# Sums of squares on all four column groups, and a shared copy out of PSUM, in a two-layer trunk with latent attention

## The chip, the cores and the metric

The kernel runs on one core of a Trainium2 chip. The metric is the device time of one execution in microseconds (us). TensorE is written PE below, VectorE DVE, ScalarE ACT, GpSimd POOL and the queue that issues most transfers SP.

## The reference

The kernel computes two layers of a residual trunk over 528 tokens (16 meta tokens, then 512), with 1024 channels. What matters here are the three root-mean-square norms at the head of each layer:

```python
h = rmsnorm(h_res, norm_gain[l])          # over 1024 channels
proj = h @ w_in[l]
u_pool, z_pool, c_q, c_kv, k_rope, z_mla, g_pool, g_mla = split(proj)
# c_kv: 256 channels
c_kv = rmsnorm(c_kv_raw, g_kva)
...
kv = (c_kv @ w_kv_b)
merged = sigmoid(g_pool) * y_pool + sigmoid(g_mla) * y_mla
h_res = h_res + merged @ w_out[l]
```

`rmsnorm(x)` is `x * rsqrt(mean(x * x) + 1e-6) * gain`.

## The kernel before

Channels lie on the 128 partitions and tokens along the free dimension, so that a sum over channels is a matmul with ones. The token axis of 528 is handled as two halves of 264 (`FULL`); in the second layer most products run only over the last 512 (`XTOK`).

**The stream of GEMM tiles.** All large products are split into three matmuls (high x high, high x low, low x high: lines 190 to 192) in float32r, with weights that ACT rounds (line 185, `whi`) and DVE subtracts (line 186, `wlo`). Weights come in chunks of 256 KB through three buffers each. `stream()` is a generator over the planned products; every `yield` returns the estimated time of the matmuls just emitted. Side work is put between them by hand: `fill_now(ns)` emits about `ns` nanoseconds of GEMM matmuls before the next side step is emitted. Lines 190 to 192 are therefore the ordinary matmuls of the text. A scheduler then orders each engine's instructions with a timing model of its own, so that the built order of an engine can differ a little from the order of emission.

**The norms.** The norm of x is not applied before the projection. The products run on the raw x (times gain), and `norm_sums` works out the reciprocal roots while the products go on. It is called once in each layer, after the two tiles of the kv latent (`ckv0`, `ckv1`):

- The squares of x lie in eight tiles `xsq[0..7]`, those of the latent in `csq[0..1]`, each 128x528. Line 363 sums them with f32 matmuls against 32 columns of ones. `tile_position` chooses one of four column groups of 32 (0, 32, 64, 96) of PE. Sums of x go to groups 0 (first half of the tokens) and 64 (second half), those of the latent to 32 and 96. There is one PSUM tile for each half.
- ACT copies the two sums out of PSUM (line 370, 64x264 each). DVE replicates the meta tokens' part (line 371).
- Five transposes (lines 375 and 376) turn the sums so that tokens lie on partitions; each moves 33 columns, of which the first and the last are used.
- DVE adds the epsilons (lines 381 to 383) and takes three Newton steps to the reciprocal root (lines 294 to 300), then splits it (lines 391 to 393).
- `rows` transposes it back (lines 404 to 407, the row transposes of the text), and ACT copies it into `kinv` (lines 409, 410).
- `spread` (line 286) replicates each root over 128 partitions with a matmul, and ACT copies it out (line 287): two halves of `rinv`, for x, and two halves of `cinv`, for the latent. The eviction of the first product that needs `rinv` is that of `u0` (line 491), the first that needs `cinv` is that of `k0` (line 574).

The matmul tiles in PSUM, these spreads among them, come from one pool of four banks (`mmt`), so that a spread may have to wait until ACT has copied an earlier one.

The rotary key's product (`kr_body`, line 430) is elsewhere in the layer; it uses all four column groups with 16 f32 matmuls of 264 columns, and one PSUM tile for each half.

The order of products after the sums is `cq1`, `cq2` (three `cq` tiles start a layer's queue, the first before the sums), `u0`, `k0`, `u1`, the rotary key, `k1`, and so on.

Of the kernel before, what the change touches and what calls it, by code (L numbers as in the profile page):

```python
# [9 lines left out]
F32 = mybir.dt.float32  # L10
# [3 lines left out]
AF = mybir.ActivationFunctionType  # L14
ALU = mybir.AluOpType
# [3 lines left out]
P = 128  # L19
DEPTH = 2  # L20
D = 1024
SEQ = 512
NM = 16
T = SEQ + NM
HALF = T // 2
# [46 lines left out]
def trunk(ctx, tc, xT, pos, win, wkr, wqb, wkb, wvb, wgr, wpu, wmu, wout, gains, const, yT):  # L72
    nc = tc.nc
    pe, act, dve, gp, sp = nc.tensor, nc.scalar, nc.vector, nc.gpsimd, nc.sync
# [5 lines left out]
    sm = ctx.enter_context(tc.tile_pool(name="sm", bufs=1))  # L80
# [5 lines left out]
    def nm(s):  # L86
        uid[0] += 1
        return f"{s}_{uid[0]}"

    def slot(tag, dt=F32, bufs=1, w=W):  # L90
        return sl.tile([P, w], dt, tag=tag, name=nm(tag), bufs=bufs)

    def tmp(w=W):
        return tp.tile([P, w], F32, tag="tmp", name=nm("tmp"), bufs=3)
# [4 lines left out]
    def mmt():  # L99
        return pp.tile([P, 512], F32, tag="mm", name=nm("mm"), bufs=4)  # L100

    def sct():
        return pp.tile([P, 512], F32, tag="S", name=nm("S"), bufs=3)
# [27 lines left out]
    ident = cst[:, C_ID:C_ID + P]  # L131
    ones = cp.tile([P, P], F32, name="ones")
# [109 lines left out]
    def step():  # L242
        c = next(main, None)
        if c is None:
            flush()
            return False
        clk[0] += c
        while pend and pend[0][0] <= clk[0]:
            pend.pop(0)[1]()
        return True  # L250
# [23 lines left out]
    def fill_now(ns):  # L274
        end = clk[0] + ns
        while clk[0] < end and step():
            pass
# [5 lines left out]
    def spread(dst, i):  # L283
        for a, b in FULL:
            ps = mmt()[:, :b - a]
            pe.matmul(ps, sel[0:34, i:i + 1].to_broadcast([34, P]), kinv[:, a:b], start=True, stop=True)
            act.activation(dst[:, a:b], ps, AF.Copy)

    def behind(ins, other):
        tc.add_manual_dep(ins.ins, other.ins.name,  # L290
                          mybir.DependencyInfo(mybir.DependencyClass.Sync, mybir.DependencyReason.DATA))

    def newton(y, a, t):
        dve.tensor_single_scalar(y.bitcast(I32), a.bitcast(I32), 1, op=ALU.logical_shift_right)
        dve.tensor_scalar(y.bitcast(I32), y.bitcast(I32), -1.0, float(0x5F3759DF), op0=ALU.mult, op1=ALU.add)
        dve.tensor_scalar(a, a, -0.5, None, op0=ALU.mult)
        for _ in range(3):
            dve.tensor_mul(t, y, y)
            dve.tensor_mul(t, t, a)
            dve.scalar_tensor_tensor(out=y, in0=t, scalar=1.5, in1=y, op0=ALU.add, op1=ALU.mult)  # L300
# [20 lines left out]
    class Layer:  # L321
# [32 lines left out]

        def norm_sums(self):
            fill_now(2600)
            ps = [mmt(), mmt()]
            for t, r, start, stop in [(self.xsq[k], 0, k == 0, k == 7) for k in range(6)] + [
                    (self.csq[0], 32, True, False), (self.xsq[6], 0, False, False),
                    (self.xsq[7], 0, False, True), (self.csq[1], 32, False, True)]:  # L360
                for s, (a, b) in enumerate(FULL):
                    r_ = r + 64 * s
                    mm = pe.matmul(ps[s][r_:r_ + 32, :HALF], ones[:, 0:32], t[:, a:b], start=start, stop=stop,  # L363
                                   tile_position=(0, r_))
                    if t is not self.csq[1]:
                        behind(mm, self.csq_last)
            sums = tmp()
            rep = sm.tile([64, 8, NM], F32, tag="rep", name=nm("rep"))
            for s, (a, b) in enumerate(FULL):
                act.activation(sums[0:64, a:b], ps[s][64 * s:64 * s + 64, :HALF], AF.Copy)  # L370
            dve.tensor_copy(rep, sums[0:64, 0:NM].unsqueeze(1).to_broadcast([64, 8, NM]))
            fill_now(2600)
            ps = mmt()[:, 0:165].rearrange("p (j c) -> p j c", c=33)
            for j in range(4):
                pe.transpose(ps[:, j, :], sums[0:33, NM + P * j:NM + P * (j + 1)], ident[0:33, 0:33])
            pe.transpose(ps[:, 4, :], rep[0:33].rearrange("p a b -> p (a b)"), ident[0:33, 0:33])
            na = sm.tile([P, 2, 5], F32, tag="na2", name=nm("na2"))
            nt = sm.tile([P, 2, 5], F32, tag="nt2", name=nm("nt2"))
            self.ninv = ny = sm.tile([P, 2, 5], F32, tag="ny2", name=nm("ny2"))
            self.eps = sm.tile([P, 5], F32, tag="eps", name=nm("eps"))  # L380
            dve.tensor_scalar(na[:, 0, :], ps[:, :, 0], 1.0 / D, EPS, op0=ALU.mult, op1=ALU.add)
            dve.tensor_scalar(self.eps, na[:, 0, :], EPS, None, op0=ALU.mult)
            dve.scalar_tensor_tensor(out=na[:, 1, :], in0=ps[:, :, 32], scalar=1.0 / 256, in1=self.eps,
                                     op0=ALU.mult, op1=ALU.add)
            newton(ny, na, nt)
            w = tmp()
            gp.memset(w[:, 0:170], 0.0)
            v = w[:, 0:170].rearrange("p (j c) -> p j c", c=34)
            nv = ny.rearrange("p a j -> p j a")
            nh = sm.tile([P, 5, 2], F32R, tag="nh", name=nm("nh"))  # L390
            dve.tensor_copy(nh, nv)
            dve.tensor_copy(v[:, :, 0:33:32], nh.bitcast(F32))
            dve.tensor_sub(v[:, :, 1:34:32], nv, nh.bitcast(F32))
            fill_now(8200)
            self.rows(v, 34, kinv)
            self.inv, self.cinv = slot("rinv"), slot("cq9")
            fill_now(1300)
            spread(self.inv, 0)
            spread(self.cinv, 1)
            self.st = [sct(), sct()]  # L400
# [719 lines left out]
```

## Time and profile before

| | |
|---|---|
| median of three runs | 800.36 us (799.65 to 800.38) |
| the profiled execution | 799.36 us |
| its span, first to last instruction | 797.6 us |
| PE busy | 790.3 us, 99% of the span |
| line 363, both layers | 80 records of 386 ns, 40 in each layer |
| granted PE clock | 1.00 |

How to read it: the span is what the engines' rows cover; the execution is 1.8 us longer. In the timeline a row gives the start, the time from the first start to the last end of the merged instructions, the engine, the line, the operation, output and inputs, sizes and count, and in brackets how long the engine stood idle before it and what released it. Matmuls overlap in the pipeline, so that the record of one (0.28 us for 264 columns) is longer than the step from one start to the next. Times are counted from the first instruction. DVE, ACT and POOL run beside PE; their time counts only where PE waits for it.

### The profile page before, as it was taken

How to read it: one execution, taken by the hardware profiler on the slowest of the kernel's cores; microseconds unless marked ns; L12 is line 12 of the kernel's file. 1: busy time of each engine (PE TensorE's matmuls, PEld its weight loads, DVE VectorE, ACT ScalarE, POOL GpSimd, SP SyncE). 2: the span in 40 equal slices, each digit the busy share in tenths (PEclk: the TensorE clock that was granted, in tenths of full speed). 3: DMA queues.
4: the chain of work that ended last, by engine and by line, in shares of the span. 5: the costliest groups of instructions: out<-in, count | busy, mean ns of one | idle time of the engine just before them, and what ended most of it. 6: DMA issues, size and time to landing. Idle time of an engine off the chain costs nothing.

```text
span 797.6 us, 14595 instructions
## 1 busy us (share of the span) xinstructions
PE 790.3 (99%) x5329; PEld 711.8 (89%) x5329; DVE 528.1 (66%) x1136; ACT 416.0 (52%) x943; POOL 194.4 (24%) x262
## 2 busy tenths in 40 slices
PE   9999999999999999999999999999999999999998
PEld 8889999999999999999997997877788888887887
DVE  5568767437689987685354686665467889665942
ACT  8455645644556665543354456446455666654421
POOL 1024404003333322142000163021024333410600
PEclk9999999999999999999999999999999999999999
DMA  6222233335233222324642222334252322222373
GB/s 241 74 70 91 72 100 90 110 86 146 79 88 89 79 67 67 89 87 145 179 142 73 73 88 87 94 84 119 81 165 89 101 83 78 71 70 77 93 225 105
DMA packets 48872, 80.71 MB, mean 101 GB/s; under 512 B 5904, under 2 KB 14480, under 8 KB 48800
## 3 DMA queue, kind: packets, MB, share of 16 engines
q1 hardware_dynamic: 48656, 79.52, 33.2%
q8 instruction: 42, 0.69, 0.4%
q10 hardware_dynamic: 144, 0.26, 0.1%
q14 instruction: 30, 0.25, 0.1%
HBM read 73.40 MB, written 4.23 MB: 97 GB/s over the span
## 4 chain that ended last, share of the span: by engine, by line
PE 96%; DMA 2%; ACT 1%; DVE 1%; issue 0%; POOL 0%; ACTq 0%; POOLq 0%
PE mm L190 28%; PE mm L192 27%; PE mm L191 27%; PE mm L805 2%; PE S L191 2%; PE S L192 2%; PE S L190 1%; PE o L811 1%; PE o L810 1%; PE mm L363 1%; PE S L472 1%; DMA xb<-xT 1%; DMA bc<-kdr 1%; PE mm L430 0%; DMA rinv<-win 0%; DMA raw<-wmu 0%
## 5 line engine op out<-in xcount | busy, mean ns | idle before, releaser
L190 PE MATMUL mm<-hh,whi 128*128 128x264 f32 (+2 forms) x1096 | 346.0, 318 | 0.5 <-ACT whi L185 0.3
L191 PE MATMUL mm<-hl,whi 128*128 128x264 f32 (+2 forms) x1096 | 343.4, 314 | 0.0
L192 PE MATMUL mm<-hh,wlo 128*128 128x264 f32 (+2 forms) x1096 | 342.1, 315 | 0.0
L186 DVE TENSOR_TENSOR wlo<-raw,whi 128x512 fp32r<-128x512 f32 (+2 forms) x251 | 186.5, 746 | 115.0 <-ACT whi L185 108.2
L185 ACT ACTIVATE whi<-raw 128x512 fp32r<-128x512 f32 (+2 forms) x251 | 150.2, 601 | 182.6 <-PE mm L191 136.9
L190 PEld LDWEIGHTS mm<-hh,whi 128*128 128x128 f32 x1096 | 205.6, 188 | 13.8 <-ACT racc L819 0.5
L191 PEld LDWEIGHTS mm<-hl,whi 128*128 128x128 f32 x1096 | 206.2, 188 | 12.2 <-issue 0.4
L192 PEld LDWEIGHTS mm<-hh,wlo 128*128 128x128 f32 x1096 | 205.0, 188 | 12.7 <-issue 0.4
L711 POOL TENSOR_TENSOR tmp<-kp,bc 64x528 f32<-64x528 f32 x16 | 24.5, 1530 | 115.0 <-DMA bc<-kdr 79.8
L550 POOL TENSOR_TENSOR racc<-racc,tmp 128x264 f32<-128x264 f32 (+1 forms) x15 | 14.1, 941 | 142.8 <-ACT tmp L549 142.7
L783 POOL TENSOR_TENSOR pm<-pa,rs 128x16 f32<-128x16 f32 x32 | 11.6, 363 | 143.9 <-DVE rs L778 143.9
L893 POOL TENSOR_TENSOR tmp<-tmp,xb 128x264 f32<-128x264 f32 (+1 forms) x24 | 27.1, 1152 | 58.1 <-DVE tmp L891 33.0
L739 DVE CUSTOM_DVE_ANT_0 S<-S,maskw,nqs 128x272 f32<-128x272 f32 (+4 forms) x80 | 38.4, 498 | 1.6 <-PE S L192 1.2
L746 ACT ACTIVATE cq<-S,bia 128x400 f32<-128x400 f32 (+2 forms) x48 | 24.6, 517 | 22.0 <-DVE bia L773 12.2
L190 PE MATMUL mm<-u,whi 128*128 128x264 f32 (+1 forms) x108 | 35.2, 326 | 0.0
L192 PE MATMUL mm<-cq,wlo 128*128 128x264 f32 (+1 forms) x108 | 34.8, 323 | 0.0
L192 PE MATMUL mm<-u,wlo 128*128 128x264 f32 (+1 forms) x108 | 34.8, 322 | 0.0
L191 PE MATMUL mm<-cq,whi 128*128 128x264 f32 (+1 forms) x108 | 34.7, 322 | 0.0
L190 PE MATMUL mm<-cq,whi 128*128 128x264 f32 (+1 forms) x108 | 34.7, 322 | 0.0
L281 DVE TENSOR_TENSOR tl<-mm,th 128x512 fp32r<-128x512 f32 (+1 forms) x64 | 29.3, 481 | 6.8 <-ACT th L280 5.8
L785 POOL TENSOR_TENSOR cq<-cq,rs 128x384 f32<-128x384 f32 (+1 forms) x32 | 32.4, 1012 | 0.0
L280 ACT ACTIVATE th<-mm 128x512 fp32r<-128x512 f32 (+1 forms) x64 | 25.5, 433 | 10.3 <-PE mm L805 10.0
(266 smaller groups left out, 1374.4 us busy)
## 6 DMA issues: line engine op xcount, KB each, us to landing
raw<-win SPq DMA_DIRECT2D x143, 256.0 KB, 2.6
raw<-wout SPq DMA_DIRECT2D x32, 256.0 KB, 3.1
bc<-kdr SPq DMA_DIRECT2D x16, 264.0 KB, 3.7
raw<-wpu SPq DMA_DIRECT2D x16, 256.0 KB, 2.7
raw<-wmu SPq DMA_DIRECT2D x16, 256.0 KB, 2.6
raw<-wqb SPq DMA_DIRECT2D x12, 256.0 KB, 2.7
tmp<-xT SPq DMA_DIRECT2D x16, 132.0 KB, 3.3
tmp<-scr SPq DMA_DIRECT2D x7, 256.0 KB, 3.5
```

What stands on the lines that cost most here:

```text
L185: act.activation(hi[:, :n], raw[:, :n], AF.Copy)
L186: dve.tensor_sub(lo[:, :n], raw[:, :n], hi[:, :n].bitcast(F32))
L190: pe.matmul(out, wh, xh, start=start, stop=False)
L191: pe.matmul(out, wh, xl, start=False, stop=False)
L192: pe.matmul(out, wl, xh, start=False, stop=stop)
L280: act.activation(hi[:, a:b], src, AF.Copy)
L281: dve.tensor_sub(lo[:, a:b], src, hi[:, a:b].bitcast(F32))
L711: gp.tensor_mul(kf[r0:r0 + 64, :], self.kp[r0:r0 + 64, :], bc[r0:r0 + 64, :])
L739: dve.tensor_tensor_reduce(out=sv, in0=sv, in1=mask, scale=nqs[:, i, h:h + 1], scalar=3e38, op0=ALU.add, op1=ALU.min, accum_out=bia[:, c:c ...
L746: act.activation(pv, sv, AF.Exp, scale=-1.0, bias=bia[:, i:i + 1], accum_out=rs[:, c:c + 1])
L785: gp.tensor_mul(pt[i][:, NM:], pt[i][:, NM:], rs[:, i:i + 1].to_broadcast([P, n - NM]))
L893: gp.tensor_add(t[:, :b - a], t[:, :b - a], self.am[m][:, a:b])
```

## The change

- The sums of x are dealt out over all four column groups by the number of the tile: even tiles to groups 0 (first half of the tokens) and 64 (second half), odd tiles to 32 and 96. The eight tiles share one PSUM tile `px`. The latent's two tiles are dealt out in the same way into a second PSUM tile `pc`, so that each sum now comes as two partial sums. The emission takes two tiles at a time and goes through the four groups in turn.
- ACT copies the sums of x to partitions 0 to 63 of `sums`, DVE those of the latent to partitions 64 to 127. The replication covers 128 partitions instead of 64.
- The five transposes move 97 columns instead of 33. The first four are made to wait for ACT's last copy.
- DVE adds the partial sums with two further small operations.
- In the first layer 3900 ns of GEMM matmuls instead of 2600 are emitted between the sums and the transposes (half of a 264-column GEMM tile more).

```diff
         def norm_sums(self):
             fill_now(2600)
-            ps = [mmt(), mmt()]
-            for t, r, start, stop in [(self.xsq[k], 0, k == 0, k == 7) for k in range(6)] + [
-                    (self.csq[0], 32, True, False), (self.xsq[6], 0, False, False),
-                    (self.xsq[7], 0, False, True), (self.csq[1], 32, False, True)]:
+            px, pc = mmt(), mmt()
+            runs = [(px, self.xsq[k], k, k < 2, k >= 6) for k in range(8)] + [(pc, self.csq[m], m, True, True) for m in range(2)]
+            for k in range(0, 10, 2):
                 for s, (a, b) in enumerate(FULL):
-                    r_ = r + 64 * s
-                    mm = pe.matmul(ps[s][r_:r_ + 32, :HALF], ones[:, 0:32], t[:, a:b], start=start, stop=stop,
-                                   tile_position=(0, r_))
-                    if t is not self.csq[1]:
-                        behind(mm, self.csq_last)
+                    for ps, t, m, start, stop in runs[k:k + 2]:
+                        g = 64 * s + 32 * (m % 2)
+                        mm = pe.matmul(ps[g:g + 32, :HALF], ones[:, 0:32], t[:, a:b], start=start, stop=stop,
+                                       tile_position=(0, g))
+                        if t is not self.csq[1]:
+                            behind(mm, self.csq_last)
             sums = tmp()
-            rep = sm.tile([64, 8, NM], F32, tag="rep", name=nm("rep"))
+            rep = sm.tile([P, 8, NM], F32, tag="rep", name=nm("rep"))
             for s, (a, b) in enumerate(FULL):
-                act.activation(sums[0:64, a:b], ps[s][64 * s:64 * s + 64, :HALF], AF.Copy)
-            dve.tensor_copy(rep, sums[0:64, 0:NM].unsqueeze(1).to_broadcast([64, 8, NM]))
-            fill_now(2600)
-            ps = mmt()[:, 0:165].rearrange("p (j c) -> p j c", c=33)
+                copied = act.activation(sums[0:64, a:b], px[64 * s:64 * s + 64, :HALF], AF.Copy)
+                dve.tensor_copy(sums[64:128, a:b], pc[64 * s:64 * s + 64, :HALF])
+            dve.tensor_copy(rep, sums[:, 0:NM].unsqueeze(1).to_broadcast([P, 8, NM]))
+            fill_now(2600 if self.l else 3900)
+            ps = mmt()[:, 0:485].rearrange("p (j c) -> p j c", c=97)
             for j in range(4):
-                pe.transpose(ps[:, j, :], sums[0:33, NM + P * j:NM + P * (j + 1)], ident[0:33, 0:33])
-            pe.transpose(ps[:, 4, :], rep[0:33].rearrange("p a b -> p (a b)"), ident[0:33, 0:33])
+                behind(pe.transpose(ps[:, j, :], sums[0:97, NM + P * j:NM + P * (j + 1)], ident[0:97, 0:97]), copied)
+            pe.transpose(ps[:, 4, :], rep[0:97].rearrange("p a b -> p (a b)"), ident[0:97, 0:97])
...
             dve.tensor_scalar(na[:, 0, :], ps[:, :, 0], 1.0 / D, EPS, op0=ALU.mult, op1=ALU.add)
+            dve.scalar_tensor_tensor(out=na[:, 0, :], in0=ps[:, :, 32], scalar=1.0 / D, in1=na[:, 0, :],
+                                     op0=ALU.mult, op1=ALU.add)
             dve.tensor_scalar(self.eps, na[:, 0, :], EPS, None, op0=ALU.mult)
-            dve.scalar_tensor_tensor(out=na[:, 1, :], in0=ps[:, :, 32], scalar=1.0 / 256, in1=self.eps,
-                                     op0=ALU.mult, op1=ALU.add)
+            for c in (64, 96):
+                dve.scalar_tensor_tensor(out=na[:, 1, :], in0=ps[:, :, c], scalar=1.0 / 256,
+                                         in1=self.eps if c == 64 else na[:, 1, :], op0=ALU.mult, op1=ALU.add)
```

In the changed file the lines after the diff stand four further down: the row transposes are lines 408 to 411, the copies into `kinv` lines 413 and 414, the spreads stay at 286 and 287, the transposes of the sums are lines 376 and 377, DVE's copies out of PSUM line 371, the replication line 372, and the additions of the epsilons and partial sums lines 382 to 387.

## The prediction

> **What bounds the kernel now.** I read the page first: busy shares and the chain that ended last.
>
> ```profile
> span 797.6 us, 14595 instructions
> ...
> PE 790.3 (99%) x5329; PEld 711.8 (89%) x5329; DVE 528.1 (66%) x1136; ACT 416.0 (52%) x943; POOL 194.4 (24%) x262
> ...
> PE 96%; DMA 2%; ACT 1%; DVE 1%; issue 0%; POOL 0%; ACTq 0%; POOLq 0%
> ```
>
> TensorE is busy nearly throughout and is 96% of the chain: time taken off its queue comes off the end, and work elsewhere costs only where TensorE waits for it. Next, the timeline of TensorE around the sums of squares of layer 0 (line 363), around the rotary key's matmuls (line 430), which already use four column groups, and around the spreads of the reciprocal roots (line 286) in both layers.
>
> ```profile
> 24.07 0.28 PE L192 MATMUL mm<-hh,wlo 128*128 128x264 f32 x1
> 24.28 1.97 PE L363 MATMUL mm<-cq,ones 128*32 128x264 f32 x16
> 26.09 1.95 PE L363 MATMUL mm<-q,ones 128*32 128x264 f32 x24
> 28.54 0.25 PE L375 MATMUL mm<-cst,tmp 33*128 33x33 f32 x1 [0.50 <-ACT tmp L370]
> 28.71 0.39 PE L190 MATMUL mm<-hh,whi 128*128 128x264 f32 x1
> 28.94 0.28 PE L191 MATMUL mm<-hl,whi 128*128 128x264 f32 x1
> ...
> 41.80 0.63 PE L286 MATMUL mm<-kinv,sel 34*128 34x264 f32 x3
> 42.91 0.39 PE L286 MATMUL mm<-kinv,sel 34*128 34x264 f32 x1 [0.48 <-ACT rinv L287]
> ...
> 56.37 0.28 PE L192 MATMUL mm<-hh,wlo 128*128 128x264 f32 x1
> 56.58 1.99 PE L430 MATMUL mm<-xb,raw 128*32 128x264 f32 x32
> 58.50 0.39 PE L190 MATMUL mm<-kh,whi 128*128 128x264 f32 x1
> 58.72 0.28 PE L191 MATMUL mm<-kl,whi 128*128 128x264 f32 x1
> ...
> 448.37 0.51 PE L286 MATMUL mm<-kinv,sel 34*128 34x264 f32 x2
> 448.81 0.39 PE L192 MATMUL mm<-hh,wlo 128*128 128x264 f32 x1
> 449.04 0.29 PE L190 MATMUL mm<-hh,whi 128*128 128x264 f32 x1
> ```
>
> Each f32 matmul is two records. To price an interruption I count from the last ordinary matmul before it to the second after it, less the ordinary cadence: 0.1215 us for 264 columns (66 steps from 31.80 to 39.84), 0.2315 us for 512. So line 430 takes 58.72 - 56.37 - 0.24 = 2.11 us for 16 matmuls. Line 363 in layer 1, where nothing is waited for, takes 3.89 us for 20 (426.77 to 431.12, less two steps of 0.23). Both fit one rule: 0.44 us for each matmul of the busiest column group plus 0.36 at the edges (4 x 0.44 and 8 x 0.44).
>
> **The change, part by part.**
>
> Column groups. Today groups 0 and 64 each take eight matmuls of x while 32 and 96 take two of the latent; afterwards each group takes five: 5 x 0.44 + 0.36 = 2.56 us, 1.33 less in each layer. Bounds: 16 to 20 in proportion to line 430 gives 2.64, so 2.4 to 2.9.
>
> The Trainium skill's page TensorEngine Tiling (Array Packing), section Overview (Theoretical Speedup), gives up to 2x for 64 and 4x for 32 columns. By that factor two groups becoming four would halve the 3.89 us, and the whole sum below would be 3.7 instead of 2.4 us. The rows speak for less: line 363 already puts its latent matmuls into the idle groups.
>
> The wait. In layer 0 the first transpose stands right behind the sums and waits 0.50 us for the ACT copy. In the changed kernel's built order it stands 24 ordinary matmuls later, the other four after two more. The sums end at 24.19 + 2.56 = 26.75 on the old clock; ACT's two copies (0.80 together) end near 27.5. DVE's two new copies of 64x264 I take at 0.43 each (a PSUM read of 128x264, line 491; bounds 0.22, the 64x128 copy of line 371, and 0.69), so they and the replication end by 28.0. The transposes come at 26.75 + 24 x 0.1215 = 29.67, so even copies of 0.69 stay hidden. The wait goes, 0.50. In layer 1 the copies end near 430.8 and the transposes come at 434.4; there was no wait.
>
> Transposes. Five of 33 columns in one group cost 0.63 (435.52 to 436.61, less two steps); the row transposes, four of 128 columns and one of 16, cost 0.66. The new width of 97 lies between. In layer 0 they were already split in two (0.25 and 0.56) and stay so: 0.30 and 0.60, +0.09. In layer 1 the built order puts one ordinary matmul between the first and the rest: 0.30 + 0.60 instead of 0.63, +0.27 (bounds +0.1 and +0.4).
>
> The Trainium skill's page TensorEngine Tiling, section Tiling Modes (Key Properties), says that a change of tiling mode drains the engine. It speaks against the new split and gives no time; the trace's price for entering and leaving is about 0.2 us.
>
> DVE's chain to the roots. It gains two small operations at 0.20 us, and in both layers the built order lets weight splits (line 186) and a latent's eviction pass between them. DVE is no bound; what matters is that the result is there when TensorE reaches the row transposes. Layer 0: transposes done 30.8, five operations and the first three of the root 1.4, weight split at 32.65 (its ScalarE half waits for the buffer freed near 31.9), then two more interruptions: done near 37.2, needed at 30.81 + 70 x 0.1215 = 39.32. Layer 1: start 435.55, held by a split until 437.3 and an eviction until 438.2, done near 441.7, needed at 444.4. The trace has small operations stretched to 0.78 and 1.31 us in these chains; one more such still fits. Cost 0; beyond 2 us of lateness it would count fully.
>
> Spreads, layer 0. All four follow the first half of u0 now. Before, three and the wait of 0.48 for the first copy took 1.63 us (41.59 to 43.46, less two steps). ACT had been busy until 42.5; it will be idle. They come at 39.32 + 0.68 for the row transposes + 24 x 0.1215 = 42.92. First spread 43.01, first copy 43.44 to 43.83, fourth spread 43.88, second copy ends 44.11 and frees the bank of the next matmul, at 44.20: 1.28 us. So -0.35 (bounds -0.5 and 0).
>
> Spreads, layer 1: the part against the change. Before, seven ordinary matmuls stood between the first and second pair, and each pair cost about 0.64 without a wait. The built order leaves one. The third and fourth spread reuse the banks of the first and second and wait for ScalarE's copies; and ahead of these copies ScalarE now has a weight split (0.63 us) that waits for the matmul just before the first spread. ScalarE's lines before:
>
> ```profile
> 448.80 0.67 ACT L287 ACTIVATE rinv<-mm 128x264 f32<-128x264 f32 x2 [0.36 <-PE mm L286]
> 449.89 0.63 ACT L185 ACTIVATE whi<-raw 128x512 fp32r<-128x512 f32 x1 [0.43 <-ACT rinv L287]
> 450.43 0.65 ACT L287 ACTIVATE cq<-mm 128x264 f32<-128x264 f32 x2
> ```
>
> By hand: the sums end at 427.00 + 2.56 = 429.56, the transposes and 48 matmuls of 512 columns at 441.57, and 23 matmuls, the row transposes (0.66) and 24 matmuls later, at 447.93, one matmul is left of u0; split 448.15 to 448.78, copies end 449.08 and 449.36; third spread 449.13, its copy ends 449.95 and frees the bank that k0 needs: k0 starts at 450.05. That is 2.0 us instead of 1.28, +0.72 (bounds 0, if ScalarE is on time, and +1.0).
>
> Everything else (POOL's memset and addition changing places, the wider replication at the same 128 free elements, the extra 1.3 us of emission ahead) is beside TensorE; SP's queue is unchanged. Outside these two stretches the order and its waits are the same, so a lead is kept.
>
> Sum. Layer 0: -1.33 - 0.50 + 0.09 - 0.35 = -2.09. Layer 1: -1.33 + 0.27 + 0.72 = -0.34. Together -2.4 us; the profiled execution (799.36, span 797.6 and 1.8 around it) would become 797.0. It is 1.0 below the median of the runs, 800.36, so I predict 798.0.
>
> **Rivals.**
> 1. The gain is mostly eaten by waits. If layer 1's spreads cost the bound of +1.0, layer 0's save nothing and the sums take 2.9, the gain falls by 0.28 + 0.35 + 0.68 to 1.1: 799.3. For it: the wait already seen at 42.91. Against: in layer 0 the copies' engine is idle when the spreads come.
> 2. The four groups do not overlap as hoped (both latents and all of x now write few banks), and the sums stay at 3.89. Then 0.76 is left in layer 0 and layer 1 loses 0.99: 800.6. Against it: line 430's four groups write one bank and run at 2.11 for 16.
> 3. Slower: DVE's chain becomes the bound. It decides once the roots come over 2.1 (layer 0) or 2.7 us (layer 1) later than I reckon, since TensorE then stands at the row transposes, in order, with all of u0 or half of it queued behind. Two small operations, two copies and the splits that now pass between them would have to stretch as the 1.31 us row does, four or five times in each layer; 4.5 us past the slack in sum gives +2.1: 802.5. For it: a small operation that normally takes 0.17 did take 1.31. Against: one in each chain did.
> 4. Throughput doubles with the number of groups in turn, whatever they hold: each block falls to half of 3.89, 0.61 less than I take: gain 3.7, 796.7. For it: two of today's groups are nearly idle. Against it: line 430's 2.11 for 16 matmuls, more than half of 3.89.
>
> **How the numbers follow.** Forecast 0.67, rival 1 0.17, rival 2 0.05, rival 3 0.06, rival 4 0.05. About 0.2%, 1.6 us, is what a measurement of this kernel can tell from no change. Forecast and rival 4 lie beyond it: faster 0.72. Rivals 1 and 2 lie within: same 0.22. Rival 3: slower 0.06. The range: best bounds of sums, spreads and transposes together with a scatter of the medians of some 0.4 us (the runs span 799.65 to 800.38) reach 796.8; the worse end takes in half of rival 1, to 799.5.
>
> **What would show it.** In the changed profile: line 363's 40 records of a layer within about 2.4 us, no idle before the transposes, none before the row transposes; in layer 0 k0's first matmul near 47.1 (was 49.17); in layer 1 a wait for line 287 before the third spread and before k0, and the stretch from the sums to k0 only 0.3 us shorter. Wrong if line 363 stays over 3 us, if TensorE waits for DVE at line 408, or if layer 1's lead is a full 1.3 us or negative.

## The result, and the profile after

The changed kernel takes 796.99 us (median of six runs, 796.48 to 798.12) against 800.17 us before (six runs, 799.65 to 800.44): the ratio is 0.9962, interval 0.9949 to 0.9975, so it is 0.4% or 3.2 us faster. Its profiled execution took 796.48 us. From the page of the changed kernel, span, busy shares and chain:

```profile
span 794.7 us, 14602 instructions
...
PE 787.5 (99%) x5329; PEld 711.2 (89%) x5329; DVE 530.0 (67%) x1144; ACT 415.6 (52%) x943; POOL 194.2 (24%) x262
...
PE 96%; DMA 1%; ACT 1%; DVE 0%; POOL 0%; issue 0%; SPq 0%; ACTq 0%; POOLq 0%
```

The count of PE's instructions is the same, and PE's busy time fell by 2.8 us, nearly all of the 2.9 us by which the span fell. DVE has eight more instructions and 1.9 us more work; its share of the chain reads 0%.

The timeline of PE in layer 0 shows the sums first, with the last ordinary matmul before them and the second after them; then the transposes, with the ordinary matmuls around them; then the spreads:

```profile
23.88 0.28 PE L192 MATMUL mm<-hh,wlo 128*128 128x264 f32 x1
24.09 1.10 PE L363 MATMUL mm<-cq,ones 128*32 128x264 f32 x16
25.00 1.52 PE L363 MATMUL mm<-q,ones 128*32 128x264 f32 x24
26.45 0.39 PE L190 MATMUL mm<-hh,whi 128*128 128x264 f32 x1
26.68 0.28 PE L191 MATMUL mm<-hl,whi 128*128 128x264 f32 x1
...
29.36 0.28 PE L192 MATMUL mm<-hh,wlo 128*128 128x264 f32 x1
29.48 0.25 PE L376 MATMUL mm<-cst,tmp 97*128 97x97 f32 x1
29.51 0.37 PE L190 MATMUL mm<-hh,whi 128*128 128x264 f32 x1
29.72 0.29 PE L191 MATMUL mm<-hl,whi 128*128 128x264 f32 x1
29.84 0.42 PE L376 MATMUL mm<-cst,tmp 97*128 97x97 f32 x3
30.09 0.25 PE L377 MATMUL mm<-cst,rep 97*128 97x97 f32 x1
30.12 0.37 PE L192 MATMUL mm<-hh,wlo 128*128 128x264 f32 x1
30.33 0.28 PE L190 MATMUL mm<-hh,whi 128*128 128x264 f32 x1
...
42.42 0.63 PE L286 MATMUL mm<-kinv,sel 34*128 34x264 f32 x3
43.29 0.38 PE L286 MATMUL mm<-kinv,sel 34*128 34x264 f32 x1 [0.23 <-ACT rinv L287]
```

The same 40 records now take 26.68 - 23.88 - 0.24 = 2.56 us instead of 3.89. No row of the transposes carries a bracket any more: the wait of 0.50 us is gone. The first transpose, on its own from 29.36 to 29.72 less two steps, costs 0.12 us and the other four 0.37, where the prediction had 0.30 and 0.60. The fourth spread still waits for the first copy, 0.23 instead of 0.48 us.

In layer 1 the sums take 2.56 us too (424.60 to 427.62, less two steps of 0.23), and the five transposes 0.47 (432.02 to 433.18, less three steps). The spreads are the part where the change loses; PE's timeline, then ACT's, in layer 1:

```profile
445.24 0.28 PE L191 MATMUL mm<-hl,whi 128*128 128x264 f32 x1
445.45 0.50 PE L286 MATMUL mm<-kinv,sel 34*128 34x264 f32 x2
445.88 0.39 PE L192 MATMUL mm<-hh,wlo 128*128 128x264 f32 x1
446.56 0.66 PE L286 MATMUL mm<-kinv,sel 34*128 34x264 f32 x2 [0.29 <-ACT rinv L287]
447.43 0.39 PE L190 MATMUL mm<-kh,whi 128*128 128x264 f32 x1 [0.20 <-ACT cq L287]
447.65 0.28 PE L191 MATMUL mm<-kl,whi 128*128 128x264 f32 x1
```

```profile
445.60 0.63 ACT L185 ACTIVATE whi<-raw 128x512 fp32r<-128x512 f32 x1 [0.84 <-PE mm L191]
446.14 0.65 ACT L287 ACTIVATE rinv<-mm 128x264 f32<-128x264 f32 x2
```

The weight split (line 185) has waited 0.84 us for PE's matmul just before the spreads and then stands ahead of the copies. The third spread waits for the first of these, k0 for the third. 445.24 to 447.65 less three steps is 2.05 us, against the 2.0 that the prediction took and the 1.28 before.

The stretch that holds all of this runs from the last ordinary matmul before the sums to the first product of k0 with `kl`. It fell from 25.23 to 22.88 us in layer 0 and from 23.75 to 23.05 in layer 1: 2.35 + 0.70 = 3.05 us. The span shortened by 2.9: the kernel reached its first sums 0.19 us earlier, and a wait outside these stretches (PE's S matmul at line 190 for ACT's `kh`, line 280) was 0.8 instead of 0.4 us.

### The profile page after: what moved, and what is told of

Read it like the earlier page. It is cut to its first block, busy times and chain, and to the rows that moved or that the text cites. A ratio compares the mean times of both kernels' runs of the same rounds, so it can differ in the third digit from the quotient of the medians.

```text
span 794.7 us, 14602 instructions
## 1 busy us (share of the span) xinstructions
PE 787.5 (99%) x5329; PEld 711.2 (89%) x5329; DVE 530.0 (67%) x1144; ACT 415.6 (52%) x943; POOL 194.2 (24%) x262
## 4 chain that ended last, share of the span: by engine, by line
PE 96%; DMA 1%; ACT 1%; DVE 0%; POOL 0%; issue 0%; SPq 0%; ACTq 0%; POOLq 0%
PE mm L190 28%; PE mm L192 28%; PE mm L191 28%; PE mm L809 2%; PE S L191 2%; PE S L192 2%; PE S L190 2%; PE o L815 1%; PE o L814 1%; PE S L476 1%; DMA bc<-kdr 1%; PE mm L363 1%; DMA raw<-win 1%; PE mm L434 0%; PE mm L820 0%; ACT whi L185 0%
```

## The experiments

"The kernel" in the expectations is the changed one, and a span of 794.7 is its span.

**Two groups of x in turn, not all four at once.** The same share for each group, but tiles 0 to 3 go to groups 0 and 64 and tiles 4 to 7 to 32 and 96, with the halves innermost, so that neighbours in the queue share two groups:

```diff
-            runs = [(px, self.xsq[k], k, k < 2, k >= 6) for k in range(8)] + ...
+            runs = [(px, self.xsq[k], k, k % 4 == 0, k % 4 == 3) for k in range(8)] + ...
...
-                        g = 64 * s + 32 * (m % 2)
+                        g = 64 * s + 32 * (m // 4 if ps is px else m)
```

> The changed kernel with the same 20 matmuls per layer on the same four column groups, but dealt out so that only two groups are in turn at a time: tiles 0 to 3 go to groups 0 and 64, tiles 4 to 7 to 32 and 96. Theory (matmuls of one group follow each other at 0.44 us, only neighbours in the queue on other groups run beside them): eight matmuls in a row on a pair of groups, about 8.2 x 0.44 + 0.36 = 4.0 us for the sums of a layer instead of 2.56, so about 2.9 us longer in all. Rival (each group's total alone matters, five each, or a fixed price per matmul): 2.56 us and no change in the time.

Measured: one run, 798.18 us (before, on the same chip: 799.78), span 796.4. The sums take 3.48 us in layer 1 (425.37 to 429.31, less two steps) and 3.47 in layer 0. That lies between the two expectations. PE's timeline in layer 1 says why:

```profile
425.69 1.31 PE L363 MATMUL mm<-cq,ones 128*32 128x264 f32 x10
426.62 0.42 PE L363 MATMUL mm<-q,ones 128*32 128x264 f32 x2
426.83 0.39 PE L363 MATMUL mm<-cq,ones 128*32 128x264 f32 x2
...
427.31 1.73 PE L363 MATMUL mm<-q,ones 128*32 128x264 f32 x18
```

Records named `cq` are the tiles 0 to 3, on groups 0 and 64. Those named `q` are the later ones: tiles 4 to 7, on 32 and 96, and last the latent's two. In the built order, which here is that of the emission, they stand behind all of the `cq` ones. The first `q` records start at 426.62, ahead of `cq` records that start at 426.83, 427.05 and 427.27. So PE does reach past matmuls whose group is busy, but only so far: the second pair of groups starts 0.93 us after the first, and 0.93 + 5 x 0.44 + 0.35 for the edges is the 3.48. The share of each group alone is therefore not enough; going through the four groups in turn, as the change does, is worth 3.48 - 2.56 = 0.92 us in each layer.

**97 rows in the kernel before.** The kernel before with the transposes widened to 97 rows, the additional ones zeros:

```diff
+            gp.memset(sums[64:128, :], 0.0)
-            rep = sm.tile([64, 8, NM], F32, tag="rep", name=nm("rep"))
+            rep = sm.tile([P, 8, NM], F32, tag="rep", name=nm("rep"))
...
-                pe.transpose(ps[:, j, :], sums[0:33, ...], ident[0:33, 0:33])
+                pe.transpose(ps[:, j, :], sums[0:97, ...], ident[0:97, 0:97])
```

> The kernel before with nothing changed but the width of the five transposes of the sums: 97 rows instead of 33 (the rows added are zeros set by GpSimd). Theory (a transpose of 33 rows takes the array out of its full-height mode and back, one of 97 rows doesn't): the transposes cost 0.47 instead of 0.63 us in layer 1 and about 0.5 instead of 0.8 beside the wait in layer 0; span about 0.4 us shorter. Rival (the price of a transpose is its columns, and the changed kernel's transposes were cheap because their operands had long been ready): 0.66 us in layer 1, span 0 to 0.1 longer.

Measured: one run, 799.51 (before: 799.78), span 797.7. PE's timeline in layer 1:

```profile
435.88 0.39 PE L192 MATMUL mm<-hh,wlo 128*128 128x512 f32 x1
436.11 0.50 PE L376 MATMUL mm<-cst,tmp 97*128 97x97 f32 x4
...
436.79 0.39 PE L191 MATMUL mm<-hl,whi 128*128 128x512 f32 x1
```

Five transposes of 97 rows and columns cost 0.45 us (less two steps of 0.23) where five of 33 cost 0.63; in layer 0 the last four cost 0.37 instead of 0.56. Three times the columns, and cheaper. The stretches to k0 became 24.96 and 23.57 us, 0.45 shorter in all, but the span did not shorten. So the same kernel was run again, timed:

> The kernel of e2_wide_before once more, timed, since its single time did not show the 0.45 us that its two stretches from the sums to k0 had become shorter. Theory: the stretches stay at 24.96 and 23.57 us, and the median lies 0.3 to 0.6 us below the kernel before. Rival (the zeros written by GpSimd or the wider copy cost elsewhere what the transposes save): the same median as before, within 0.2 us.

Measured: 799.37 us (11 runs) against 799.63 (21 runs), ratio 0.9997, interval 0.9988 to 1.0006; stretches 24.97 and 23.56. The local saving repeated. In time it is not told apart from nothing: in both profiles the wait for `kh` is longer than the 0.4 us of before (0.7 and 0.8), and that takes back most of it. The interval, down to 1.0 us shorter, does not rule the 0.45 out either. The wait lies between 0.15 and 0.85 us over all the kernels here, in no order that follows the edits. So does the start: outside one run (below), the last ordinary matmul before the first sums comes anywhere from 23.88 to 24.54 us. Both put a scatter of some tenths on each span below, and the stretches, which hold neither, are the better measure.

**The half tile taken back.** The fill ahead of the transposes as before, the rest as changed:

```diff
-            fill_now(2600 if self.l else 3900)
+            fill_now(2600)
```

> The changed kernel with 2600 ns emitted ahead of the transposes in both layers, as before (the half tile undone). The built order of layer 0 then has the first transpose right behind the sums, and the spreads five matmuls behind the row transposes instead of 24. Theory (the half tile covers the copies): the first transpose waits about 0.9 us for the copies, and the spreads up to 0.3 for ScalarE's copy of the roots; layer 0 loses 0.9 to 1.3 us, layer 1 nothing. Rival (the earlier roots are worth as much, as the spreads come in front of u0): within 0.3 us of the changed kernel.

Measured: one run, 797.32, span 795.5, 0.8 longer. In layer 0 the first transpose waits 0.59 us for ACT's copy of the sums and the fourth spread 0.48 instead of 0.23:

```profile
27.51 0.28 PE L376 MATMUL mm<-cst,tmp 97*128 97x97 f32 x1 [0.59 <-ACT tmp L370]
```

The stretch there is 23.70 instead of 22.88, in layer 1 it is unchanged (23.06). By the stretch the half tile is worth 0.8 us, the wait at the transposes and part of the one at the spreads.

**The copies all on ACT.** DVE's two copies go back to ACT, behind its own two:

```diff
-                dve.tensor_copy(sums[64:128, a:b], pc[64 * s:64 * s + 64, :HALF])
+            for s, (a, b) in enumerate(FULL):
+                copied = act.activation(sums[64:128, a:b], pc[64 * s:64 * s + 64, :HALF], AF.Copy)
```

> The changed kernel with all four copies of the sums out of PSUM on ScalarE (DVE's share undone). ScalarE's copies then end about 0.8 us later, near 28.1 in layer 0, and the transposes come at 29.5. Theory (the copies lie beside TensorE's ordinary matmuls, whoever makes them): no wait before the transposes, which stand in one group here (about 0.47 us in both layers); span within 0.4 us of the changed kernel's 794.7. Rival (DVE's share is part of the gain): a wait before the transposes and a span 0.5 us or more longer.

Measured: one run, 796.25, span 794.5; no wait before the transposes; stretches 22.83 and 23.03. By the stretches, DVE's share in the copying earns nothing once the half tile stands ahead of the transposes: both ways are hidden.

**The groups alone.** The last kernel with the shorter fill as well, so that what is left of the change is the four groups and the 97 rows:

```diff
-                dve.tensor_copy(sums[64:128, a:b], pc[64 * s:64 * s + 64, :HALF])
+            for s, (a, b) in enumerate(FULL):
+                copied = act.activation(sums[64:128, a:b], pc[64 * s:64 * s + 64, :HALF], AF.Copy)
...
-            fill_now(2600 if self.l else 3900)
+            fill_now(2600)
```

> The column groups alone: the changed kernel with ScalarE making all four copies and 2600 ns emitted ahead of the transposes in both layers. The built order of layer 0 puts four transposes right behind the sums. Theory: the sums take 2.56 us in both layers, but in layer 0 the first transpose waits for four copies, about 1.4 us; layer 1 has no wait there. Span about 1.2 us longer than the changed kernel's 794.7, so most but not all of the gain over 797.6. Rival (the cover is not needed, since what follows waits less): span within 0.4 us of 794.7.

Measured: one run, 799.75, span 798.0, 2 us longer than expected. The stretch in layer 0 is 24.52, that in layer 1 23.04, as reckoned; the rest was lost before the sums, which began some 1.6 us late. PE's timeline of this kernel near the start shows where:

```profile
7.06 0.42 PE L191 MATMUL mm<-hl,whi 128*128 128x264 f32 x1
7.28 0.42 PE L190 MATMUL mm<-hh,whi 128*128 128x264 f32 x1
```

The step is 0.22 us and stays so until 10.6; in the changed kernel's profile the same two start at 6.86 and 6.98, and in every other profile the step is 0.12 from 6.9 us on at the latest. So the kernel was run again, timed:

> The kernel of e6_groups_alone once more, timed. In its trace the matmuls of the first products ran with a step of 0.22 us for 264 columns from 6.7 to 10.6 us, where all other traces had 0.12 from 6.4 to 6.9 on: about 1.6 us that the edit would not explain. Theory (the slow start belongs to that execution): the profile starts its first sums near 23.9 to 24.6 us, the stretches from the sums to k0 stay at 24.5 and 23.0 us, and the median lies 1.6 us above the changed kernel's, about 1.5 us below the kernel before. Rival (the edit delays the start): first sums again near 25.5 us, and the median is that of the kernel before.

Measured: 798.38 us (11 runs) against 799.63 (21 runs), ratio 0.9985, interval 0.9976 to 0.9994; span 796.4, first sums after 24.07, stretches 24.52 and 23.04. The late start belonged to that one execution. So the four groups and the 97 rows alone bring 1.2 us of the 3.2, since in layer 0 the wait for the copies takes back part of what the sums save. Against the changed kernel's 0.9962 the half tile and DVE's copies together are worth about 0.0023, 1.8 us (each ratio is known to about 0.001); the stretch says 24.52 - 22.88 = 1.64. The wait is in PE's timeline in layer 0:

```profile
28.09 0.55 PE L377 MATMUL mm<-cst,tmp 97*128 97x97 f32 x4 [1.38 <-ACT tmp L372]
```

With four copies on ACT and no half tile the transposes stand 1.38 us; with the half tile alone, or with both, they do not wait; with DVE's copies alone they wait 0.59. Either of the two edits hides a part, and the half tile hides all of it.

**Other banks for the second pair of spreads.** The spreads of `cinv` take their PSUM tiles from the attention scores' pool (`sct`) instead of `mmt`:

```diff
-    def spread(dst, i):
+    def spread(dst, i, alloc):
...
-            ps = mmt()[:, :b - a]
+            ps = alloc()[:, :b - a]
...
-            spread(self.cinv, 1)
+            spread(self.cinv, 1, sct)
```

> The changed kernel with the latent's two spreads in banks of the scores' pool instead of the pool of four, so that they need not wait for ScalarE's copies of the first two. Theory (in layer 1 the waits for these copies take back 0.7 us of the gain): from the last matmul before the spreads to k0 about 1.0 us instead of 2.05 in layer 1 and 1.0 instead of 1.38 in layer 0; span about 1.3 us shorter than the changed kernel's 794.7. Rival (the wait only moves: k0 or the eviction of u0 waits for the same ScalarE, held by the weight split): a wait of 0.5 us or more in front of k0 in layer 1, span within 0.4 us of 794.7.

Measured: one run, 795.20 us, span 793.4, 1.3 shorter, as expected; the two stretches are 22.37 and 22.19, 1.37 shorter in all. PE's timeline in layer 1:

```profile
444.84 0.28 PE L191 MATMUL mm<-hl,whi 128*128 128x264 f32 x1
445.05 0.50 PE L286 MATMUL mm<-kinv,sel 34*128 34x264 f32 x2
445.40 0.40 PE L286 MATMUL S<-kinv,sel 34*128 34x264 f32 x2
445.73 0.39 PE L192 MATMUL mm<-hh,wlo 128*128 128x264 f32 x1
446.17 0.39 PE L190 MATMUL mm<-kh,whi 128*128 128x264 f32 x1
446.40 0.28 PE L191 MATMUL mm<-kl,whi 128*128 128x264 f32 x1
```

No bracket is left: the four run together. The spreads cost 1.20 us (444.84 to 446.40, less three steps) instead of 2.05 in layer 1 and 0.87 instead of 1.38 in layer 0. What made the third and fourth spread and k0 wait was the pool of four banks, and ACT's copy only because it frees a bank.

**Spreads of full height.** The last kernel, with `kinv` and `sel` filled up with zeros to 128 rows, so that the spreads contract 128 rows instead of 34:

```diff
-            pe.matmul(ps, sel[0:34, i:i + 1].to_broadcast([34, P]), kinv[:, a:b], start=True, stop=True)
+            pe.matmul(ps, sel[:, i:i + 1].to_broadcast([P, P]), kinv[:, a:b], start=True, stop=True)
```

> The changed kernel with the latent's spreads in the scores' banks, as in the run on other banks, and besides all four spreads with 128 rows instead of 34 (the added rows of both operands are zeros). Theory (34 rows change the array's row mode and back, 128 do not): in layer 0 the four spreads take about 0.5 us instead of the 0.87 of that run; in layer 1 about 0.2 less than its 1.20, as the first copy then holds k0. Span about 0.5 us shorter than its 793.4. Rival (the edges of about 0.4 us come from the copied operand or from float32r alone): 0.87 and 1.20 as there, span within 0.2 us of 793.4.

Measured: one run, 794.94 us, span 793.1, 0.3 shorter. PE's timeline in layer 0:

```profile
42.48 0.28 PE L192 MATMUL mm<-hh,wlo 128*128 128x264 f32 x1
42.60 0.28 PE L286 MATMUL mm<-kinv,sel 128*128 128x264 f32 x1
42.72 0.28 PE L286 MATMUL S<-kinv,sel 128*128 128x264 f32 x1
42.84 0.29 PE L286 MATMUL mm<-kinv,sel 128*128 128x264 f32 x1
42.97 0.28 PE L286 MATMUL S<-kinv,sel 128*128 128x264 f32 x1
43.09 0.28 PE L190 MATMUL mm<-hh,whi 128*128 128x264 f32 x1
43.21 0.28 PE L191 MATMUL mm<-hl,whi 128*128 128x264 f32 x1
```

From 42.48 on every matmul starts 0.12 or 0.13 us after the one before it: the four spreads cost 0.49 us, just the ordinary step each, where those of 34 rows cost 0.87. In layer 1 the stretch did not shorten (22.19, was 22.20): k0 now arrives early and waits 0.44 us for ACT's first copy, so there the gain turned into a wait.

**All of these together.** The same with the first row transpose at 128 rows instead of 16:

```diff
-            pe.transpose(kt1[0:n, 0:NM], v[0:NM, 4, :], ident[0:NM, 0:NM])
+            pe.transpose(kt1[0:n, 0:P], v[:, 4, :], ident)
```

> As the run with spreads of 128 rows in the scores' banks, and the first of the row transposes too takes all 128 rows instead of 16 (its spare columns are overwritten by the next one). Theory of row modes: each of the four groups of row transposes takes about 0.15 us less than 0.67, so the span is about 0.5 us shorter than that run's, near 792.4, and the ratio to the kernel before 0.993 to 0.995. Rival (no edge from 16 rows): the row transposes stay at 0.67 us and the span within 0.2 us of that run's.

Measured: 794.54 us (five runs, 794.27 to 795.58) against 800.27 (eight runs, 799.44 to 801.45), ratio 0.9932, interval 0.9918 to 0.9946; span 792.5. PE's timeline in layer 0:

```profile
39.12 0.28 PE L192 MATMUL mm<-hh,wlo 128*128 128x264 f32 x1
39.23 0.27 PE L408 MATMUL mm<-cst,tmp 128*34 128x128 f32 x1
39.34 0.49 PE L410 MATMUL mm<-cst,tmp 128*34 128x128 f32 x3
39.67 0.27 PE L411 MATMUL mm<-cst,tmp 128*34 128x128 f32 x1
39.70 0.37 PE L190 MATMUL mm<-hh,whi 128*128 128x264 f32 x1
39.90 0.29 PE L191 MATMUL mm<-hl,whi 128*128 128x264 f32 x1
```

The row transposes cost 0.54 us (39.12 to 39.90, less two steps) instead of 0.67. The kernel beats both: the changed one had 0.9962, with an interval that ends just above this one's. How much of that is the banks and how much the height is told by the stretches alone.

## Why the prediction was right, and where its sizes were off

It forecast a gain of 2.4 us and a time of 798.0; the kernel gained 3.2 by the medians and came to 796.99, inside the range and 0.2 us from its lower end. Of the 0.9 us by which the time lies under the sum (800.36 - 2.43), 0.6 stands in the two stretches, and 0.2 in the median before, which came down to 800.17 with three more runs. The lower end was tighter than its own bounds: those of the sums (0.32 in both layers), of the spreads (0.15 and 0.72) and of layer 1's transposes (0.17) add up to 1.36 us, which reaches 796.6 before any scatter.

- **Column groups: exact.** 2.56 us in both layers, as taken. The rule of 0.44 us for each matmul of the busiest group plus the edges holds, and the first experiment adds its condition, the order of emission. Neither rival on the groups came true. The median lies nearer to the 796.7 of rival 4, in which each block halves, than to the forecast, but not for its reason: 2.56 us is not the 1.95 that it needs.
- **The wait: exact.** It went, as the fill was reckoned to cover it. Taking the half tile back brings a wait of 0.59 us back. DVE's copies took 0.43 us each (426 to 436 ns), as taken from line 491.
- **Transposes: mis-sized, by 0.84 us in all.** This is the term that was off. It was +0.09 and +0.27; measured against before it was 0.49 - 0.81 = -0.32 and 0.47 - 0.63 = -0.16. The prediction put the width of 97 between the rows of 33 and of 128 columns and added the price of entering and leaving, about 0.2 us, once for each group of transposes. With 97 rows there is no such price: the second experiment shows it on the kernel before, and that a split costs nothing then. The rule that was weighed, by which a change of tiling mode drains the engine (the Trainium skill's page TensorEngine Tiling (Array Packing), section Tiling Modes (Key Properties)), may well be the cause of the edges, but no row shows a mode. It was read as speaking against the split; the rows say that 97 rows pay no edge and 33 do, so it would speak for the wider transposes.
- **DVE's chain: right, at no cost.** In layer 0 it was done by 36.9 us (37.2 forecast) with one operation stretched to 0.76 us, in layer 1 by 439.9 with one of 1.30 us, which with the lead of 2.2 us from layer 0 (424.60 for 426.77) is 442.0 on the clock of the forecast's 441.7 and of the 444.4 at which it was needed. PE did not wait at line 408. The slower rival needed four or five such stretches in each layer.
- **Spreads.** Layer 0: 1.38 us, forecast 1.28, since the fourth still waited 0.23. Layer 1: 2.05, forecast 2.0, with both predicted waits at the predicted places. That the banks cause them, through ACT's copies, is shown by the change of pool.
- **Sum.** 2.43 + 0.84 - 0.10 - 0.05 = 3.1 us, against 3.05 measured in the two stretches. Of the predicted signs, layer 1's lead came out as 0.70 instead of 0.34, from the transposes. In layer 0 k0 began at 46.63 instead of near 47.1: 0.26 of that is the stretch, again the transposes, and 0.19 the earlier start of the sums.
- **Rival 1,** the gain mostly eaten by waits, was right for one of its three parts: the loss at layer 1's spreads came close to its bound (0.77 of 1.0), while layer 0's spreads still saved 0.25 and the sums did not rise.

The wait for `kh` is a matter of a transfer, as the changed kernel's rows for POOL, ACT and PE show:

```profile
180.09 1.77 POOL L715 TENSOR_TENSOR tmp<-kp,bc 64x528 f32<-64x528 f32 x1 [41.34 <-DMA bc<-kdr]
181.90 0.64 ACT L280 ACTIVATE kh<-tmp 128x528 fp32r<-128x528 f32 x1 [4.08 <-POOL tmp L715]
182.59 0.57 PE L190 MATMUL S<-kh,qhl 128*128 128x272 f32 x2 [0.81 <-ACT kh L280]
```

POOL waits for the transfer that reads `kdr`, a small tensor parked in device memory, back over all partitions (`bc`, issued at line 705), ACT waits for POOL, and PE for ACT. Over the twelve profiles this transfer landed 4.15 to 4.88 us after its issue, and PE's wait was 4.0 us less than that each time (0.41 with 4.43 before, 0.81 with 4.82 after, 0.15 with 4.15 where the copies are all on ACT). None of the edits touches this transfer. Open is what makes the transfer itself quicker or slower, and with that scatter what the 97 rows alone are worth in time.

## What to carry to other kernels

Small matmuls on column groups cost by the busiest group, if they are emitted so that the groups come round in turn; a fair share in a blocked order got only part of it. Price an interruption of a dense stream by its shape as well as its count: here transposes and spreads of 97 or 128 rows went in without an edge, and those of 16, 33 or 34 rows paid one, so in PE's queue filling up with zeros was cheaper than being small. The sums on column groups paid their 0.36 us of edges although they have 128 rows. When side work is pulled together in the stream, look at the pool that its outputs come from and at what stands ahead of the copies that free it: that was the one place where this change lost time, and another pool won it back.

## What the runs showed of the hardware that was not expected

- **Outside the column groups, height sets the edge.** Five transposes: 0.63 us at 33 rows, 0.45 to 0.49 at 97. Four spreads without a wait: 0.87 us at 34 rows, 0.49 at 128. The row transposes: 0.67 us with one of 16 rows among them, 0.54 with all at 128.
- **Matmuls overtake.** In the first experiment matmuls on idle column groups started 0.21 to 0.65 us ahead of earlier ones in the queue, whose group was busy. How far PE reaches past them was not tried beyond that one order.
- **The start of an execution varies.** In one execution the matmuls of 264 columns kept a step of 0.22 us until 10.6 us, in the other eleven profiles only until 6.9 at the latest: 1.6 us of span that no edit caused, while the granted clock in the profile's rows reads 1.00 throughout. By the Trainium skill's page TensorE: Matmul & The Clock Gate, Part 1 (the HAM clock gate), the array starts at half its clock and is released by a free-running window, at a point that varies by half a microsecond either way. The doubled step agrees with the half clock, though the column of the granted clock does not show it; the point of release here came 3.7 us later than in the latest of the others, which is more than the page gives. Why stays open.
